# The state update of a linear-attention chunk moved ahead of the chunk's output product

## The chip, the cores and the metric

The kernel runs on one NeuronCore of one Trainium2 chip. The metric is the device time of one execution in microseconds (us), the median over the runs shown. The engines are named as in the profile: PE (TensorE matmul), PEld (its weight loads), DVE (VectorE), ACT (ScalarE), POOL (GpSimd), SP (SyncE, which issues most DMAs). A queue name such as SPq means the engine's instruction queue.

## The reference

One decoder layer on 2048 tokens of width 1024, with 16 learned meta tokens ahead of them. After an RMSNorm, one combined input projection feeds two branches, a state-space branch (SSD, 16 heads in 4 groups, chunks of 128) and a gated linear attention (GLA, 4 heads, key width 128, value width 256); both are projected, gated, added and projected once more. The two recurrences that matter here:

```python
# GLA, one chunk (per head): S has 128 x 256
o_inter = (q * exp(g)) @ S                  # uses the state before this chunk
o_intra = att @ v
S_new   = exp(g_last)[:, None] * S + k_dec.T @ v
o       = o_inter + o_intra
# SSD: the 16 meta tokens run first, as a chunk of their own; their final
# state is the initial state of the first real chunk
y_m, s_m = ssd_chunked(meta part, chunk=16, state0=0)
y_r, _   = ssd_chunked(real part, chunk=128, state0=s_m)
```

The gate of the GLA branch is `log_sigmoid(a_lr @ gla_gate_w2 + b) / 16`, with `gla_gate_w2` of 16 x 512. The reference uses chunks of 64 for GLA; the kernel uses 128, which gives the same sums.

## The kernel before

**First phase** (until about 1558 us): the 2048 tokens are taken in 4 blocks of 512, each as 4 chunks of 128; block 0 carries the meta tokens too. A block has eight units: four SSD groups, then four GLA heads. A unit is a projection (`ssd_proj`, `gla_proj`), long runs of 128x256 and 128x512 matmuls, which `yield`s after each piece; at its end it begins a scan (`ssd_scan`, `gla_scan`), a second generator. After each piece of projection, `step()` advances every running scan by one piece. So the PE's queue holds a piece of projection, one piece of each running scan, the next piece of projection, and so on. Weights are split in two parts (`accum` makes three matmuls of each product: high by high, high by low, low by high; lines 183 to 185). In block 0 each weight tile is loaded raw by SP, its high part is made by ACT (L163) and its low part by POOL (L164), and the result is saved to DRAM for later blocks (L179).

**Second phase**: gates, branch projections and the output projection, with seven products in place of eight.

**What sets the order.** PE's and SP's instructions stand in the order in which the code is written. The order on DVE, ACT and POOL is chosen at build time by a scheduler that works on its own estimates. All queues run in order: an instruction that waits holds back everything behind it on its engine. Waits are put in when the program is built, from the accesses to each tile. Each PSUM tile is one bank (128 x 512 f32); the pool `pc` has two, `pj` and `pt` three each.

**The GLA chunk** (`gla_scan`, L778 to 793). A chunk has one bank `po`: its right half gets the key product `kdt.T @ v` (three matmuls, L782 by way of 183 to 185), its left half the attention product `atp @ v` (three matmuls) and `qg @ s_gla` (L786). Then DVE reads the right half and updates `s_gla` in place (L787), and ACT reads the left half twice (L789, L791). A piece has two chunks, so a scan runs its four chunks in two pieces.

**Meta state** (`ssd_scan`, L512 to 517 and L580 to 588). In block 0 the piece that computes the meta state (L515, copied to SBUF by DVE L517) goes on, without a `yield`, into `before(1)` (transposes, L538) and `after(0)`, whose matmul L563 reads that state.

**Late constants** (L330 to 338). The GLA gate's weights `w2` and the masks `msk` are loaded by `late_constants()`: three DMAs of 16x512 (L333) into a tile of the tag `acc`, which has two buffers and which the convolution uses (L477 writes it, L481 reads it last), one DMA of the masks (L337), a copy on ACT (L334) and two instructions on DVE (L335, L338). It is called between the first and the second unit of block 0.

Of the kernel before, what the change touches and what calls it, by code (L numbers as in the profile page):

```python
# [7 lines left out]
F32 = mybir.dt.float32  # L8
# [4 lines left out]
ALU = mybir.AluOpType  # L13

P = 128
D = 1024
KT = 8
META = 16
BLK = 512
NCH = BLK // P  # L20
SG = 4
# [6 lines left out]
NACT = 8  # L28
# [12 lines left out]
def trunk_kernel(ctx: ExitStack, tc: tile.TileContext, xm, xmt, w_feat, w_tok, w_zm, w_br, w_o,  # L41
                 cf32, cmsk, pvec, fnw, hvec, gw2, out):
    nc = tc.nc
# [5 lines left out]
    def mk(pool, shape, dt, tag, **kw):  # L49
        cnt[0] += 1  # L50
        return pool.tile(shape, dt, tag=tag, name=f"{tag}_{cnt[0]}", **kw)
# [124 lines left out]
    def save(n):  # L176

        while len(unsaved) > n:
            nc.sync.dma_start(*unsaved.pop(0))  # L179

    def accum(ps, stat, mov, first, last, **kw):
        (sh, sl), (mh, ml) = stat, mov
        nc.tensor.matmul(ps, sh, mh, start=first, stop=False, **kw)  # L183
        nc.tensor.matmul(ps, sh, ml, start=False, stop=False, **kw)  # L184
        nc.tensor.matmul(ps, sl, mh, start=False, stop=last, **kw)  # L185
# [142 lines left out]
    msk = const.tile([P, NMSK, P], U8, name="msk")  # L328

    def late_constants():  # L330
        w2r = mk(wk, [P, META + BLK], F32, "acc")[:48, :512]
        for i in range(3):
            nc.sync.dma_start(w2r[16 * i:16 * i + 16, :], gw2)  # L333
        nc.scalar.activation(w2, w2r, AF.Copy)  # L334
        nc.vector.tensor_tensor(w2[32:48], w2r[32:48], w2[32:48].bitcast(F32), op=ALU.subtract)  # L335
        mstg = mk(wk, [P, D], F32, "tok4", bufs=NT4)[:, :NMSK * P]
        nc.sync.dma_start(mstg, cmsk)  # L337
        nc.vector.tensor_copy(msk.rearrange("p l t -> p (l t)"), mstg)  # L338
# [109 lines left out]
    def ssd_proj(o, g):  # L448
        m0, tt = o.m0, o.tt
        feats = []  # L450
        zs = mk(wk, [P, NCH, 256], F32, "tok4", bufs=NT4)
        if g == 0:
            pss = [bank(*pl) for pl in [(pj, "pj")] * 3 + [(pt, "pt")] + ([(pc, "pc")] if m0 else [])]
            yield from proj_tok("zm", w_zm, o.u, o.starts + [0] * o.ci0, list(enumerate(pss)), 288, 1, 256)
            begin(dt_chain(o, pss[NCH:] + pss[:NCH]))
            done = [(ps[:, :256], zs[:, c]) for c, ps in enumerate(pss[:NCH])]
        else:
            pss, places = halves_of(pj, "pj")
            yield from proj_tok(f"z{g}", w_tok[g], o.u, o.starts, places)
            done = [(ps, zs[:, 2 * r:2 * r + 2].rearrange("p c f -> p (c f)")) for r, ps in enumerate(pss)]  # L460
        for ps, dst in done:
            nc.scalar.activation(dst, ps, AF.Tanh, scale=0.5)
            nc.vector.scalar_tensor_tensor(dst, dst, 1.0, ps, op0=ALU.add, op1=ALU.mult)
        yield
        for j in range(4):
            ti = g * 4 + j
            pss = proj_feat(f"s{ti}", w_feat[T_SSD + ti], o.segs_all, o.mov)
            cin = mk(wk, [P, 3 + META + BLK], F32, "cin")
            acc = mk(wk, [P, META + BLK], F32, "acc")[:, :tt]
            nc.scalar.activation(cin[:, 0:3], tails[:, ti, :], AF.Copy)  # L470
            for ps, (a, n) in zip(pss, o.segs_all):
                nc.scalar.activation(cin[:, 3 + a:3 + a + n], ps[:, :n], AF.Copy)
                nc.scalar.activation(acc[:, a:a + n], ps[:, :n], AF.Identity, scale=hcw[:, ti, 3:4],  # L473
                                     bias=hcb[:, ti:ti + 1])
            nc.gpsimd.tensor_copy(tails[:, ti, :], cin[:, tt:tt + 3])
            for k in range(3):
                nc.vector.scalar_tensor_tensor(acc, cin[:, k:k + tt], hcw[:, ti, k:k + 1], acc,  # L477
                                               op0=ALU.mult, op1=ALU.add)
            f = mk(wk, [P, META + BLK], F32, "act", bufs=NACT)
            nc.scalar.activation(f[:, :tt], acc, AF.Tanh)  # L480
            nc.vector.scalar_tensor_tensor(f[:, :tt], f[:, :tt], 1.0, acc, op0=ALU.add, op1=ALU.mult)  # L481
            feats.append(f)
            yield
        begin(ssd_scan(o, g, feats, zs))

    cbs = {}
# [5 lines left out]
    def ssd_scan(o, g, feats, zs):  # L492
# [20 lines left out]
        def meta_state():  # L513
            ps = bank(pc, "pc")
            nc.tensor.matmul(ps[:, :256], btm[:META], xw[:META].rearrange("p a c -> p (a c)"),  # L515
                             start=True, stop=True)
            nc.vector.tensor_copy(s_ssd[:, g], ps[:, :256])  # L517
# [62 lines left out]
        yield  # L580
        if m0:
            meta_state()
        for c in range(1, NCH):
            before(c)
            after(c - 1)
            yield
# [15 lines left out]
    def gla_proj(o, h):  # L602
        m0 = o.m0
        t0 = T_GLA + 4 * h
        qs = mk(wk, [P, META + BLK], F32, "act", bufs=NACT)
        ps, = proj_feat(f"g{t0}", w_feat[t0], o.segs_real, o.mov)
        nc.scalar.activation(qs[:, :BLK], ps, AF.Copy, scale=QSCALE)
        yield
        kf = mk(wk, [P, META + BLK], F32, "act", bufs=NACT)
        for ps, (a, n) in zip(proj_feat(f"g{t0 + 1}", w_feat[t0 + 1], o.segs_all, o.mov), o.segs_all):  # L610
            nc.scalar.activation(kf[:, a:a + n], ps[:, :n], AF.Copy)
        yield
        vh = mk(wk, [P, NCH, 256], F32R, "tok4", bufs=NT4)
        vl = mk(wk, [P, NCH, 256], F32R, "tok4", bufs=NT4)
        vm = None
        pss, places = halves_of(pj, "pj")
        if m0:
            vm = mk(wk, [P, 256], F32, "c1", bufs=NC1)[:META]
            pv5 = bank(pt, "pt")
            places.append((2, pv5[:, :256]))  # L620
        yield from proj_tok(f"v{h}", w_tok[SG + h], o.u, o.starts + [0] * o.ci0, places)
        if m0:
            nc.scalar.activation(vm, pv5[:META, :256], AF.Copy)
        for r, ps in enumerate(pss):
            split(*[t[:, 2 * r:2 * r + 2].rearrange("p c f -> p (c f)") for t in (vh, vl)], ps)
        yield
        gs = []
        for j in range(2):
            ps, = proj_feat(f"g{t0 + 2 + j}", w_feat[t0 + 2 + j], o.segs_real, o.mov)
            gg = mk(wk, [P, BLK], F32, "gg", bufs=4)  # L630
            nc.scalar.activation(gg, ps, AF.Tanh, scale=0.5)
            nc.vector.scalar_tensor_tensor(gg, gg, 1.0, ps, op0=ALU.add, op1=ALU.mult)
            gs.append(gg)
            yield
        begin(gla_scan(o, h, qs, kf, (vh, vl), vm, gs))

    def gla_scan(o, h, qs, kf, vt, vm, gs):
# [140 lines left out]

        ot = mk(wk, [P, NCH, 256], F32, "ot", bufs=1)
        ssq = mk(sm, [P, 4], F32, "ssq")  # L780
        for c in range(NCH):
            po = bank(pc, "pc")  # L782
            vc = [t[:, c] for t in vt]
            accum(po[:, 256:], [t[:, c] for t in kdt], vc, True, True)
            accum(po[:, :256], [t[:, c] for t in atp], vc, True, False)
            nc.tensor.matmul(po[:, :256], qg[:, c * P:(c + 1) * P], s_gla[:, h], start=False, stop=True)  # L786
            nc.vector.scalar_tensor_tensor(s_gla[:, h], s_gla[:, h], egl[:, c:c + 1], po[:, 256:],  # L787
                                           op0=ALU.mult, op1=ALU.add)
            nc.scalar.activation(ot[:, c], po[:, :256], AF.Copy)  # L789
            jk = mk(wk, [P, 256], BF16, "junk", bufs=1)  # L790
            nc.scalar.activation(jk, po[:, :256], AF.Square, accum_out=ssq[:, c:c + 1])  # L791
            if c % 2:
                yield
# [19 lines left out]
    def step():  # L813
        running.extend(begun)
        begun.clear()
        for gen in list(running):
            if next(gen, running) is running:
                running.remove(gen)
# [7 lines left out]
    with tc.manual_schedule(engines={mybir.EngineType.PE, mybir.EngineType.SP}):  # L826
        for b in range(nblk):
            o = new_block(b, next_u[b])
            for i in range(SG + GH):
                if (b, i) in beside:  # L830
                    begin(beside_unit(beside[b, i]))
                if (b, i) == (0, 1):
                    late_constants()
                if i == 1:
                    begin(gates(o))
                if i == SG and b + 1 < nblk:
                    begin(fetch_u(b + 1))
                for _ in ssd_proj(o, i) if i < SG else gla_proj(o, i - SG):
                    step()
            save(0)  # L840
        while running or begun:
            step()
# [329 lines left out]
```

## Time and profile before

| what | value |
|---|---|
| time, median of 3 runs | 2348.6 us (2342.61 to 2350.83) |
| the profiled execution's own time | 2353.29 us |
| its span, first to last instruction | 2351.5 us |
| PE busy | 2251.0 us, 96% |
| DVE, ACT, POOL busy | 1547.5 (66%), 1181.6 (50%), 672.9 us (29%) |
| granted TensorE clock, mean | 0.982 |

The page of the profile gives busy time by engine and the costliest groups. A row of the waits reads: engine, line and tile of the instruction that waited, an arrow, what released it, then the total in us, how many times, and the longest. A row of the timeline reads: start, length, engine, line, operation, tile written, arrow, tiles read, shape, count, and in brackets the idle time of the engine just before it with its releaser. A row of the windows gives, for one stretch, its length, then busy time and number of instructions by engine, the granted TensorE clock (1.00 is full speed), the DMA share and GB/s. Matmul lengths overlap: in a run of 128x256 products one starts every 0.12 us and lasts 0.28 us.

### The profile page before, as it was taken

How to read it: one execution, taken by the hardware profiler on the slowest of the kernel's cores; microseconds unless marked ns; L12 is line 12 of the kernel's file. 1: busy time of each engine (PE TensorE's matmuls, PEld its weight loads, DVE VectorE, ACT ScalarE, POOL GpSimd, SP SyncE). 2: the span in 40 equal slices, each digit the busy share in tenths (PEclk: the TensorE clock that was granted, in tenths of full speed). 3: DMA queues.
4: the chain of work that ended last, by engine and by line, in shares of the span. 5: the costliest groups of instructions: out<-in, count | busy, mean ns of one | idle time of the engine just before them, and what ended most of it. 6: DMA issues, size and time to landing. Idle time of an engine off the chain costs nothing.

```text
span 2351.5 us, 36473 instructions
## 1 busy us (share of the span) xinstructions
PE 2251.0 (96%) x12641; PEld 1962.2 (83%) x12641; DVE 1547.5 (66%) x2895; ACT 1181.6 (50%) x2758; POOL 672.9 (29%) x681
## 2 busy tenths in 40 slices
PE   7799999999999999999999999879999999999998
PEld 7689889889888988888988898768878788888786
DVE  5576665676675567566568655674578854778866
ACT  5565655465534455543456443464455454554543
POOL 4343433122321212221122200207423354423331
PEclk9899999999999999999999999989999999999999
DMA  7665875666786676777677654447577876777753
GB/s 270 225 206 184 299 252 193 204 218 223 240 274 191 205 223 219 238 258 224 194 225 221 205 174 157 154 135 254 194 242 261 297 236 203 251 272 252 254 165 122
DMA packets 301545, 518.05 MB, mean 220 GB/s; under 512 B 27696, under 2 KB 143664, under 8 KB 301360
## 3 DMA queue, kind: packets, MB, share of 16 engines
q1 hardware_dynamic: 200400, 402.84, 52.9%
q10 hardware_dynamic: 100960, 112.88, 13.8%
q8 instruction: 99, 1.62, 0.3%
q14 instruction: 86, 0.70, 0.1%
HBM read 368.42 MB, written 147.19 MB: 219 GB/s over the span
## 4 chain that ended last, share of the span: by engine, by line
PE 48%; DMA 6%; DVE 6%; ACT 3%; issue 2%; SPq 1%; POOL 1%; ACTq 0%; DVEq 0%; POOLq 0%
PE pj L183 6%; PE pj L185 6%; PE pj L184 6%; PE psa L183 4%; PE psa L185 4%; PE psa L184 4%; PE psb L184 2%; PE psb L185 2%; PE psb L183 2%; DVE b L893 1%; DMA br<-br_t 1%; PE psc L183 1%; PE psc L185 1%; PE psc L184 1%; PE pc L562 1%
## 5 line engine op out<-in xcount | busy, mean ns | idle before, releaser
L183 PE MATMUL pj<-u,whl 128*128 128x512 f32 (+1 forms) x1184 | 447.9, 378 | 10.5 <-ACT whl L163 3.5
L185 PE MATMUL pj<-u,whl 128*128 128x512 f32 (+1 forms) x1184 | 431.8, 365 | 0.8 <-POOL whl L164 0.8
L184 PE MATMUL pj<-u,whl 128*128 128x512 f32 (+1 forms) x1184 | 430.8, 364 | 0.0
L183 PE MATMUL pj<-whl,u 128*128 128x256 f32 (+1 forms) x992 | 290.3, 293 | 8.2 <-ACT whl L163 6.7
L185 PE MATMUL pj<-whl,u 128*128 128x256 f32 (+1 forms) x992 | 283.4, 286 | 1.5 <-DVE u L298 1.4
L184 PE MATMUL pj<-whl,u 128*128 128x256 f32 (+1 forms) x992 | 283.4, 286 | 1.0 <-POOL whl L164 1.0
L183 PEld LDWEIGHTS pj<-u,whl 128*128 128x128 f32 x1184 | 225.9, 191 | 48.8 <-ACT whl L163 3.9
L183 PE MATMUL psa<-b,a 128*128 128x512 f32 x640 | 249.8, 394 | 11.1 <-ACT sn L930 8.2
L185 PEld LDWEIGHTS pj<-u,whl 128*128 128x128 f32 x1184 | 224.9, 190 | 36.9 <-POOL whl L164 1.1
L184 PEld LDWEIGHTS pj<-u,whl 128*128 128x128 f32 x1184 | 225.5, 190 | 33.6
L185 PE MATMUL psa<-b,a 128*128 128x512 f32 x640 | 251.3, 393 | 1.2 <-DVE a L914 1.2
L184 PE MATMUL psa<-b,a 128*128 128x512 f32 x640 | 251.0, 392 | 0.0
L183 PEld LDWEIGHTS pj<-whl,u 128*128 128x128 f32 x992 | 191.2, 193 | 9.4 <-ACT whl L163 6.9
L184 PEld LDWEIGHTS pj<-whl,u 128*128 128x128 f32 x992 | 191.0, 193 | 2.1 <-POOL whl L164 1.6
L185 PEld LDWEIGHTS pj<-whl,u 128*128 128x128 f32 x992 | 190.8, 192 | 2.2 <-DVE u L298 2.2
L893 DVE TENSOR_TENSOR b<-br,b 128x512 fp32r<-128x512 f32 x196 | 153.1, 804 | 56.2 <-ACT b L892 55.7
L80 POOL TENSOR_TENSOR wr<-wr 128x256 f32<-128x256 f32 x80 | 65.1, 814 | 425.5 <-DMA wr<-y 169.7
L904 POOL TENSOR_TENSOR as<-ar,ar 128x512 f32<-128x512 f32 x40 | 57.8, 1446 | 447.5 <-DMA ar<-in_w_br 191.2
L164 POOL TENSOR_TENSOR whl<-wr,whl 128x512 fp32r<-128x512 f32 (+1 forms) x100 | 132.9, 1335 | 182.5 <-ACT whl L163 155.2
L892 ACT ACTIVATE b<-br 128x512 fp32r<-128x512 f32 x196 | 119.2, 626 | 112.3 <-DMA br<-br_t 41.5
L914 DVE TENSOR_TENSOR a<-ar,a 128x512 fp32r<-128x512 f32 x160 | 131.8, 839 | 64.4 <-ACT a L913 64.1
L477 DVE SCALAR_TENSOR_TENSOR acc<-cin,hcw,acc 128x512 f32<-128x512 f32 (+1 forms) x192 | 154.6, 805 | 27.0 <-ACT acc L473 26.3
(271 smaller groups left out, 5062.7 us busy)
## 6 DMA issues: line engine op xcount, KB each, us to landing
whl<-k_s SPq DMA_DIRECT2D x96, 512.0 KB, 4.5
whl<-k_g SPq DMA_DIRECT2D x96, 512.0 KB, 4.2
whl<-k_v SPq DMA_DIRECT2D x48, 512.0 KB, 3.7
whl<-k_z SPq DMA_DIRECT2D x36, 512.0 KB, 3.8
wr<-in_w_feat SPq DMA_DIRECT2D x64, 256.0 KB, 4.2
k_s<-whl SPq DMA_DIRECT2D x32, 512.0 KB, 3.7
cb<-cumd ACTq DMA_DIRECT2D x64, 256.0 KB, 5.4
y<-gg ACTq DMA_DIRECT2D x64, 256.0 KB, 4.5
```

The source lines that it names most:

```text
L80: nc.gpsimd.tensor_tensor(o, x, y, op=ALU.subtract)
L164: nc.gpsimd.tensor_tensor(hl[:, 1], raw, hl[:, 0].bitcast(F32), op=ALU.subtract)
L183: nc.tensor.matmul(ps, sh, mh, start=first, stop=False, **kw)
L184: nc.tensor.matmul(ps, sh, ml, start=False, stop=False, **kw)
L185: nc.tensor.matmul(ps, sl, mh, start=False, stop=last, **kw)
L477: nc.vector.scalar_tensor_tensor(acc, cin[:, k:k + tt], hcw[:, ti, k:k + 1], acc, op0=ALU.mult, op1=ALU.add)
L562: nc.tensor.matmul(py[:, h * 64:(h + 1) * 64], dm[:, h], xdt[:, h], start=True, stop=True)
L892: nc.scalar.activation(t[:, 0], raw, AF.Copy)
L893: nc.vector.tensor_tensor(t[:, 1], raw, t[:, 0].bitcast(F32), op=ALU.subtract)
L904: nc.gpsimd.tensor_tensor(s1, a21, a22, op=ALU.add)
L914: nc.vector.tensor_tensor(t[:, 1], src, t[:, 0].bitcast(F32), op=ALU.subtract)
```

## The change

Three edits. In the GLA chunk, the DVE update is issued right after the key product, and it writes a second buffer `st`; the two buffers change roles with each chunk, and the chunk's `qg` product reads the old one. In block 0's SSD scans, the meta state is a piece of its own (a `yield` more). `late_constants()` is called within the first unit of block 0, after that unit's second piece, and its staging tile takes a buffer of the tag `act` (eight buffers).

```diff
     def late_constants():
-        w2r = mk(wk, [P, META + BLK], F32, "acc")[:48, :512]
+        w2r = mk(wk, [P, META + BLK], F32, "act", bufs=NACT)[:48, :512]
...
         if m0:
             meta_state()
+            yield
         for c in range(1, NCH):
             before(c)
             after(c - 1)
...
         ot = mk(wk, [P, NCH, 256], F32, "ot", bufs=1)
         ssq = mk(sm, [P, 4], F32, "ssq")
+        states = [s_gla[:, h], mk(wk, [P, 256], F32, "st", bufs=1)]
         for c in range(NCH):
             po = bank(pc, "pc")
             vc = [t[:, c] for t in vt]
+            old, new = states[c % 2], states[1 - c % 2]
             accum(po[:, 256:], [t[:, c] for t in kdt], vc, True, True)
+            nc.vector.scalar_tensor_tensor(new, old, egl[:, c:c + 1], po[:, 256:], op0=ALU.mult, op1=ALU.add)
             accum(po[:, :256], [t[:, c] for t in atp], vc, True, False)
-            nc.tensor.matmul(po[:, :256], qg[:, c * P:(c + 1) * P], s_gla[:, h], start=False, stop=True)
-            nc.vector.scalar_tensor_tensor(s_gla[:, h], s_gla[:, h], egl[:, c:c + 1], po[:, 256:],
-                                           op0=ALU.mult, op1=ALU.add)
+            nc.tensor.matmul(po[:, :256], qg[:, c * P:(c + 1) * P], old, start=False, stop=True)
             nc.scalar.activation(ot[:, c], po[:, :256], AF.Copy)
...
-                if (b, i) == (0, 1):
-                    late_constants()
...
-                for _ in ssd_proj(o, i) if i < SG else gla_proj(o, i - SG):
+                for n, _ in enumerate(ssd_proj(o, i) if i < SG else gla_proj(o, i - SG)):
                     step()
+                    if (b, i, n) == (0, 0, 1):
+                        late_constants()
```

In the changed kernel lines move by one or two: L787 is L788 there, L786 is L790, L654 is L655, L659 is L660, L681 is L682, L789 and L791 are L791 and L793.

**PE at the second chunk of the first GLA scan.** Each row is an instruction with its output and inputs; in brackets stands the engine on whose counter it waits (`DVE_49` counts DVE's instructions, `PE_49` PE's own, `Activation_49` ACT's). Before:

```order
L183 MATMUL pc_4101<-tok_455_3080,kdt_3665 128x256 [waits PE_49]
L184 MATMUL pc_4101<-tok_456_3081,kdt_3665 128x256
L185 MATMUL pc_4101<-tok_455_3080,kdt_3666 128x256
L183 MATMUL pc_4101<-tok_455_3080,atp_3983 128x256 [waits Activation_49]
L184 MATMUL pc_4101<-tok_456_3081,atp_3983 128x256
L185 MATMUL pc_4101<-tok_455_3080,atp_3984 128x256 [waits DVE_49]
L786 MATMUL pc_4101<-s_gla,act_3555 128x256 [waits DVE_49]
```

And of the change:

```order
L183 MATMUL pc_4102<-tok_451_3064,kdt_3649 128x256 [waits PE_49]
L184 MATMUL pc_4102<-tok_452_3065,kdt_3649 128x256
L185 MATMUL pc_4102<-tok_451_3064,kdt_3650 128x256
L183 MATMUL pc_4102<-tok_451_3064,atp_3983 128x256 [waits DVE_49,Activation_49]
L184 MATMUL pc_4102<-tok_452_3065,atp_3983 128x256
L185 MATMUL pc_4102<-tok_451_3064,atp_3984 128x256
L790 MATMUL pc_4102<-st_4089,act_3548 128x256
```

The matmuls are the same. L786's wait for the previous chunk's update is gone; the first attention product (the second L183) now waits for DVE. The count for which it waits is reached by L788, the update of the same chunk; it is so in all 64 chunks.

**DVE around the same scan's updates.** Before:

```order
L681 TENSOR_TENSOR sq_4367<-g_all_384 128x512 [waits DVE_49]
L787 SCALAR_TENSOR_TENSOR s_gla<-s_gla,egl_3553,pc_4089 128x256 [waits PE_49]
L654 TENSOR_TENSOR act_4113<-act_4113,act_3567 128x528 [waits Activation_49]
L787 SCALAR_TENSOR_TENSOR s_gla<-s_gla,egl_3553,pc_4101 128x256 [waits PE_49]
L659 TENSOR_TENSOR act_4125<-act_4125,act_3489 128x512 [waits Activation_49]
L787 SCALAR_TENSOR_TENSOR s_gla<-s_gla,egl_3553,pc_4204 128x256 [waits PE_49]
```

And of the change:

```order
L682 TENSOR_TENSOR sq_4368<-g_all_384 128x512 [waits DVE_49]
L788 SCALAR_TENSOR_TENSOR st_4089<-s_gla,egl_3546,pc_4090 128x256 [waits PE_49]
L655 TENSOR_TENSOR act_4114<-act_4114,act_3560 128x528 [waits Activation_49]
L788 SCALAR_TENSOR_TENSOR s_gla<-st_4089,egl_3546,pc_4102 128x256 [waits DVE_49,PE_49]
L660 TENSOR_TENSOR act_4126<-act_4126,act_3472 128x512 [waits Activation_49]
L788 SCALAR_TENSOR_TENSOR st_4089<-s_gla,egl_3546,pc_4205 128x256 [waits DVE_49,PE_49]
```

The updates stand at the same places of DVE's queue: behind the next head's decay work (L682), and with an instruction between them that waits for ACT (L655).

**ACT in the first unit of block 0**, where the first projection's outputs (`pj`, `pt`, `pc`) are read and the next weights (`whl`) are split. Before:

```order
L163 ACTIVATE whl_522<-wr_524 128x288 [waits DMAHW0_49,DMAHW5_49,PE_49,Pool_49]
L163 ACTIVATE whl_591<-wr_593 128x512 [waits DMAHW4_49,DMAHW7_49,PE_49,Pool_49]
L462 ACTIVATE tok_39_386<-pj_387 128x256 [waits PE_49]
L462 ACTIVATE tok_39_386<-pj_388 128x256 [waits PE_49]
L373 ACTIVATE alr_385<-pj_387 128x48 [waits DVE_49]
```

And of the change:

```order
L334 ACTIVATE w_374<-act_589 48x512 [waits DMAHW7_49,DMAHW6_49,DMAHW0_49]
L462 ACTIVATE tok_39_386<-pj_387 128x256 [waits PE_49]
L462 ACTIVATE tok_39_386<-pj_388 128x256 [waits PE_49]
L373 ACTIVATE alr_385<-pj_387 128x48 [waits DVE_49]
L462 ACTIVATE tok_39_386<-pj_389 128x256 [waits PE_49]
L373 ACTIVATE alr_385<-pj_388 128x48 [waits DVE_49]
L462 ACTIVATE tok_39_386<-pt_390 128x256 [waits PE_49]
L373 ACTIVATE alr_385<-pj_389 128x48 [waits DVE_49]
L373 ACTIVATE alr_385<-pt_390 128x48 [waits DVE_49]
L373 ACTIVATE alr_385<-pc_391 128x48 [waits DVE_49]
L377 ACTIVATE de_578<-dx_567 128x80
L163 ACTIVATE whl_600<-wr_602 128x512 [waits DMAHW4_49,DMAHW3_49,Pool_49]
```

The copy of `w2` (L334) stands where the split of the next weight tile (`whl_591` before, `whl_600` now) stood; that split is now behind all reads of the first projection. On SP the four DMAs of `late_constants` now stand ahead of the first of these weight tiles' loads.

## The prediction

> **What bounds the kernel now.** First the page: the span and the busy time by engine.
>
> ```profile
> span 2351.5 us, 36473 instructions
> PE 2251.0 (96%) x12641; PEld 1962.2 (83%) x12641; DVE 1547.5 (66%) x2895; ACT 1181.6 (50%) x2758; POOL 672.9 (29%) x681
> ```
>
> PE is busy for 2251.0 of 2351.5 us, so only 100.5 us of idle time can be won, and whatever makes PE wait anew is paid almost in full. Next the waits of PE, of which three rows belong to the three edits: weights that came late (10.1), the GLA product that waited for the state (5.6) and the SSD product that waited for the meta state (5.3).
>
> ```profile
> PE pj L183 <- ACT whl L163: 10.1, 2, 6.7
> PE pc L786 <- DVE s_gla L787: 5.6, 4, 3.0
> PE pc L563 <- DVE s_ssd L517: 5.3, 1, 5.3
> ```
>
> The wait that the first edit attacks is small: 5.6 us in 4 of 64 chunks. Why it is so small shows in an undisturbed chunk of the timeline:
>
> ```profile
> 434.63 0.28 PE L185 MATMUL pc<-tok,kdt 128*128 128x256 f32 x1
> 434.75 0.28 PE L183 MATMUL pc<-tok,atp 128*128 128x256 f32 x1
> 435.10 0.60 PE L786 MATMUL pc<-s_gla,act 128*128 128x256 f32 x2
> 435.35 0.47 PE L183 MATMUL pc<-tok,kdt 128*128 128x256 f32 x1
> 435.74 0.48 DVE L787 SCALAR_TENSOR_TENSOR s_gla<-s_gla,egl,pc 128x256 f32<-128x256 f32 x1 [3.04 <-PE pc L786]
> 436.27 0.70 PE L786 MATMUL pc<-s_gla,act 128*128 128x256 f32 x2
> ```
>
> DVE updates the state (435.74 to 436.22) while PE runs the next chunk's six products, and L786 needs the state only at 436.27. The update lies beside PE's work. The next view is that of line 787 itself:
>
> ```profile
> L787 DVE SCALAR_TENSOR_TENSOR s_gla<-s_gla,egl,pc x64: 462/480/482, 339.1 to 1551.6; 128x256 f32<-128x256 f32 x64
>   PE pc L786: 73.5, 38
>   ACT ot L789: 21.6, 25
> ```
>
> The second row: in 38 of 64 chunks DVE had been idle before the update; in the other 26 it came to it late. The third: ACT's copy of `po` waited 25 times for this update, though it reads the left half of the bank and the update the right half and `s_gla`. So accesses to one bank are kept in the order of the program, also when they touch different halves.
>
> **Edit 1, the state update.** In the new order DVE reads the right half of `po` before the attention product writes the left half. By the rule that the third row shows, that product must then wait for DVE; and PE's new order shows it, a wait on DVE at the first attention product, in all 64 chunks. What was beside PE's work is put between two of its products. Behind the waiting matmul stand the rest of the chunk, the next chunk of the piece and the next projection.
>
> The price where DVE is free: the key product ends at 434.63 + 0.28 = 434.91; DVE answers 0.04 us after PE's end (L786 ends at 435.70, L787 starts at 435.74); the update takes 0.48; and PE resumes 0.06 us after DVE's end, as at the first scan, where DVE ends at 339.58:
>
> ```profile
> 336.24 0.28 PE L185 MATMUL pc<-tok,kdt 128*128 128x256 f32 x1
> 338.50 0.69 DVE L681 TENSOR_TENSOR sq<-g_all 128x512 f32<-128x512 f32 x1
> 339.11 0.47 DVE L787 SCALAR_TENSOR_TENSOR s_gla<-s_gla,egl,pc 128x256 f32<-128x256 f32 x1
> 339.64 0.70 PE L786 MATMUL pc<-s_gla,act 128*128 128x256 f32 x2 [1.63 <-DVE s_gla L787]
> 339.99 0.47 PE L183 MATMUL pj<-u,whl 128*128 128x264 f32 x1
> ```
>
> So the attention product starts at 434.91 + 0.04 + 0.48 + 0.06 = 435.49 in place of 434.75: 0.74 us. After a wait PE starts again slower: L786 takes 339.99 - 339.64 = 0.35 us to the next matmul's start, and 435.35 - 435.10 = 0.25 in flow, 0.10 more. I take 0.84, and 0.74 as the lower end: 64 x 0.84 = **+54** (47 at least).
>
> The price where DVE is late is more. DVE's queue is in order, and the updates stand in it behind the next head's decay work, with L655 between the first two, which waits for ACT. The second scan shows both:
>
> ```profile
> 385.55 0.28 PE L185 MATMUL pc<-tok,kdt 128*128 128x256 f32 x1
> 385.71 1.66 DVE L681 TENSOR_TENSOR sq<-g_all 128x512 f32<-128x512 f32 x1
> 387.29 0.47 DVE L787 SCALAR_TENSOR_TENSOR s_gla<-s_gla,egl,pc 128x256 f32<-128x256 f32 x1
> 390.06 0.71 DVE L654 TENSOR_TENSOR act<-act,act 128x528 f32<-128x528 f32 x1 [2.31 <-ACT act L653]
> 390.69 0.47 DVE L787 SCALAR_TENSOR_TENSOR s_gla<-s_gla,egl,pc 128x256 f32<-128x256 f32 x1
> ```
>
> The first key product ends at 385.83, but DVE comes at 387.29, 1.4 us later than a free DVE would; the second update sits behind L654 until 390.69. At the first scan DVE came at 339.11, when the key product had ended at 336.52, 2.6 us late. Before, PE saw such lateness 4 times; now it sees all of it. For the 26 late chunks I take 1.0 us each, between half of a decay instruction (0.69/2 = 0.35) and 2.6: **+26** (9 to 68). Nearer the lower end, because after a first wait DVE has caught up.
>
> The clock. The windows show what PE's idle time does to the granted clock (the clock is the third number from the end, 1.00 is full speed; the first pair after the length is PE's busy time and matmuls):
>
> ```profile
> 634.90:638.30 3.40, 1.51 (x11) 1.46 (x12) 2.69 (x6) 2.34 (x6) 2.26 (x3) 0.99 0.70 213
> 638.30:641.70 3.40, 3.40 (x16) 3.22 (x15) 2.77 (x8) 2.14 (x8) 1.47 (x2) 0.51 0.97 370
> 296.90:300.30 3.40, 1.56 (x14) 1.56 (x15) 2.02 (x2) 3.02 (x8) 3.40 (x3) 1.00 0.48 155
> 300.30:303.70 3.40, 3.40 (x31) 3.40 (x30) 3.07 (x6) 1.64 (x4) 0.58 (x1) 1.00 1.00 354
> ```
>
> After 3.4 us with 1.51 us of PE work the next 3.4 us ran at 0.51; after 1.56 us of work they ran at full clock. So a piece that idles for some 1.85 of 3.4 us also pays half of 3.4, 1.7 us. A piece's two waits where DVE is free leave about 2 x 0.6 = 1.2 us of idle, not enough; a late DVE adds the rest. I take 8 of the 32 pieces: **+14** (none, to all 32 with 54).
>
> Removed: L786's waits, **-5.6**. The writes to a second buffer and ACT's earlier start cost and win nothing: ACT is busy for 50%, and the bank that it frees is used two chunks later.
>
> [...]
>
> **Edit 2, the meta state.** The gap before L563, and what followed:
>
> ```profile
> 102.01 0.39 DVE L517 COPY s_ssd<-pc 128x256 f32<-128x256 f32 x1
> 102.46 0.80 PE L563 MATMUL pc<-s_ssd,act 128*128 128x256 f32 x1 [5.33 <-DVE s_ssd L517]
> 102.50:105.70 3.20, 3.20 (x11) 2.84 (x12) 2.96 (x8) 1.59 (x4) 0.78 (x1) 0.50 0.31 108
> ```
>
> The copy was late behind DVE's scans. With the `yield`, a piece of projection, 47 matmuls of 0.12 us by PE's new order, is put between: 5.6 us, which covers 5.33. I take all of it and the half clock behind it (3.2/2 = 1.6): **-7** (0 to -7; what is late next is the same scan's later pieces). The three other groups had no such wait, and get nothing.
>
> **Edit 3, the late constants.** SP waited for a buffer of `acc`, and the weights behind it came late:
>
> ```profile
> SPq L333 <- DVE act L481: 15.6, 1, 15.6
> 66.42 0.58 PE L183 MATMUL pj<-whl,u 128*128 128x256 f32 x1 [6.66 <-ACT whl L163]
> 67.82 0.58 PE L184 MATMUL pj<-whl,u 128*128 128x256 f32 x1 [0.82 <-POOL whl L164]
> 69.70 0.58 PE L184 MATMUL pj<-whl,u 128*128 128x256 f32 x1 [0.23 <-POOL whl L164]
> 66.40:71.60 5.20, 4.13 (x16) 3.55 (x17) 0.00 (x0) 1.26 (x2) 3.49 (x3) 0.50 0.99 366
> ```
>
> 6.66 + 0.82 + 0.23 = 7.7 us of gaps, and 5.2 us at half clock, 2.6 more: **-10.3** (at least -5, if something else in that queue is late). But the call's new place has a price. On ACT the split of the first weight tile of the next projection now stands behind all reads of the first one:
>
> ```profile
> 30.92 0.63 ACT L163 ACTIVATE whl<-wr 128x512 fp32r<-128x512 f32 x1 [2.28 <-PE pj L184]
> 31.63 1.29 POOL L164 TENSOR_TENSOR whl<-wr,whl 128x512 fp32r<-128x512 f32 x1 [2.10 <-ACT whl L163]
> 35.30 0.28 ACT L377 ACTIVATE de<-dx 128x80 f32<-128x80 f32 x1
> 33.74 0.37 PE L183 MATMUL pj<-u,whl 128*128 128x264 f32 x1
> ```
>
> PE used that tile at 33.74. L377 came at 35.30, with two splits ahead of it that now stand behind it. If it ends and the split starts at about 35.0, its low part is there at 35.0 + 0.63 + 1.29 = 36.9: a new gap of 3, and 1.7 of clock: **+4.7** (0 if ACT gets through earlier, 6 if the masks' DMA on SP delays the tile too).
>
> **Sum.** 54 + 26 + 14 - 5.6 - 7 - 10.3 + 4.7 = +75.8 on a profiled execution of 2353.29 us. That execution lies 4.7 above the median of the runs; set on the median of 2348.6 the sum gives **2424 us**, 3.2% slower.
>
> **Rivals.** (a) *The update really leaves the path.* If the attention product did not in fact wait for DVE, only the gains were left: -5.6 - 7 - 10.3 + 4.7 = -18, **2330 us**, faster. It decides if the wait for L788 costs less than 18/64 = 0.28 us a chunk. Against it: the update alone takes 0.48, and the order names the wait. For it: only that DVE is idle before 38 updates, which shortens nothing below 0.74. [...] Chance 4%. That the edits cancel to no change: 2%.
>
> (b) *Only the floor is paid.* DVE's lateness shrinks since PE's waits let it catch up, and the clock holds: 54 + 9 - 5.6 - 7 - 10.3 + 4.7 = +45, **2394 us**. For it: the 38 of 64. Against: L654's wait for ACT, which PE's waiting does not shorten. 22%.
>
> (c) *The clock falls at every piece.* Two waits close together in 3.4 us with 256-column products may count as idle enough: 32 x 1.7 = 54 in place of 14, **2464 us**. For it: in the 1.56 us window full clock was held only just. Against: a pair's 1.2 us is well short of 1.85. 16%.
>
> My forecast, 2405 to 2445, has 56%.
>
> **How the numbers follow.** Faster by over 0.3% (7 us, about what a measurement of this kernel tells from no change): 4%; within it 2%; slower 94%. The range takes in most of (b) and of (c): from 2380 (the lower ends, 47 + 9 - 5.6 - 7 - 10.3 = +33) to 2470 ((c), with 6 us more for lateness).
>
> **What would show it.** A row of PE's waits for L788 at L183 (64 waits or nearly, some 60 to 90 us with the gaps of 0.6 us each and a few of 2 to 4); L790 without a wait; the gaps at 66 and 102 us gone, one of about 3 us near 34; more slices with a lower PEclk in the first phase; the second phase (from about 1560 us before) unchanged in length. The forecast is wrong if these waits are short or few, or if the second phase moves too.

## The result, and the profile after

The changed kernel takes **2418.3 us** (median, 2411.1 to 2422.1) against 2345.6 us (2342.6 to 2350.8) of the kernel before on the same chip: a ratio of **1.0305, 95% interval 1.0281 to 1.033**. It is slower, as forecast (2424 us, 2405 to 2445 for the likeliest case). The profiled execution took 2417.06 us.

The head of the page of the changed kernel, with the span and the busy times:

```profile
span 2415.3 us, 36595 instructions
PE 2275.5 (94%) x12641; PEld 1975.7 (82%) x12641; DVE 1564.0 (65%) x2895; ACT 1185.4 (49%) x2758; POOL 677.8 (28%) x681
```

The matmuls are as many as before (12641), yet PE is busy for 24.5 us longer. The span grew by 63.8, so the other 39.3 us are idle time. Next the waits of PE after the change:

```profile
PE pc L183 <- DVE st L788: 43.5, 32, 8.4
PE pc L183 <- DVE s_gla L788: 18.0, 28, 1.3
...
PE pc L183 <- ACT junk L793: 5.0, 4, 1.8
```

The attention product's first matmul waits for the state update L788 in 60 of 64 chunks, 61.5 us in all. The other four waits at that place are put on ACT's L793, 5.0 us; two of them are 0.67 us long, as long as many waits for the update. The three rows that the edits went after (L786 for L787, L563 for L517, and `whl`) are gone from the top.

Where in the program the time went shows when the span is cut at the first GLA key product and at the first product of the second phase. The first block is the kernel before, the second the changed one; busy times and counts stand in the order PE, PEld, DVE, ACT, POOL.

```profile
0.00:336.00 336.00, 295.47 (x2082) 276.08 (x2083) 216.87 (x417) 192.89 (x480) 132.74 (x130) 0.96 0.71 241
336.00:1558.80 1222.80, 1184.81 (x7200) 1052.88 (x7198) 774.99 (x1698) 601.96 (x1563) 248.47 (x320) 0.98 0.65 207
1558.80:2351.50 792.70, 770.76 (x3360) 633.25 (x3360) 555.59 (x781) 386.78 (x716) 291.65 (x232) 0.99 0.69 232
```
```profile
0.00:319.05 319.05, 291.61 (x2082) 274.16 (x2083) 218.77 (x417) 193.13 (x480) 136.03 (x130) 0.98 0.74 253
319.05:1618.40 1299.35, 1212.01 (x7200) 1069.12 (x7198) 782.36 (x1699) 605.90 (x1563) 250.97 (x320) 0.96 0.60 195
1618.40:2415.30 796.90, 771.85 (x3360) 632.38 (x3360) 562.87 (x781) 386.38 (x716) 290.75 (x232) 0.99 0.68 230
```

The part up to the first key product, where edits 2 and 3 lie, is 17.0 us shorter. The part with the GLA chunks is **76.6 us longer** with the same 7200 matmuls: 27.2 us more busy time, at a lower mean clock (0.96 against 0.98), and 49.4 us more idle time. The second phase is 4.2 us longer.

An undisturbed piece of two chunks on PE, before the change, from its first key product to the next matmul that is not of the scan:

```profile
345.98 0.28 PE L183 MATMUL pc<-tok,kdt 128*128 128x256 f32 x1
346.33 0.28 PE L183 MATMUL pc<-tok,atp 128*128 128x256 f32 x1
...
347.47 0.28 PE L183 MATMUL pc<-tok,atp 128*128 128x256 f32 x1
...
348.39 0.27 PE L709 MATMUL pt<-cst,act 128*16 128x128 f32 x1
```

and the same piece after it:

```profile
334.91 0.28 PE L183 MATMUL pc<-tok,kdt 128*128 128x256 f32 x1
...
335.14 0.28 PE L185 MATMUL pc<-tok,kdt 128*128 128x256 f32 x1
335.99 0.39 PE L183 MATMUL pc<-tok,atp 128*128 128x256 f32 x1 [0.57 <-DVE st L788]
...
337.97 0.39 PE L183 MATMUL pc<-tok,atp 128*128 128x256 f32 x1 [0.57 <-DVE s_gla L788]
...
338.86 0.27 PE L710 MATMUL pt<-cst,act 128*16 128x128 f32 x1
```

The piece took 348.39 - 345.98 = 2.41 us and takes 338.86 - 334.91 = 3.95. That is 1.54 for two chunks, 0.77 each; from one attention product to the next it is 337.97 - 335.99 = 1.98 against 347.47 - 346.33 = 1.14 before, 0.84 more. Of the 28 two-chunk pieces ahead of the last two scans, nineteen look like this one. In the other nine DVE comes late, as in the second scan, shown here on DVE and PE of the changed kernel:

```profile
376.16 1.64 DVE L682 TENSOR_TENSOR sq<-g_all 128x512 f32<-128x512 f32 x1
377.72 0.47 DVE L788 SCALAR_TENSOR_TENSOR st<-s_gla,egl,pc 128x256 f32<-128x256 f32 x1
380.49 0.71 DVE L655 TENSOR_TENSOR act<-act,act 128x528 f32<-128x528 f32 x1 [2.30 <-ACT act L654]
381.12 0.47 DVE L788 SCALAR_TENSOR_TENSOR s_gla<-st,egl,pc 128x256 f32<-128x256 f32 x1
```
```profile
376.01 0.28 PE L185 MATMUL pc<-tok,kdt 128*128 128x256 f32 x1
378.33 0.35 PE L183 MATMUL pc<-tok,atp 128*128 128x256 f32 x1 [2.05 <-DVE st L788]
...
381.74 0.55 PE L183 MATMUL pc<-tok,atp 128*128 128x256 f32 x1 [1.32 <-DVE s_gla L788]
```

The key product was done at 376.29, but DVE stood in the next head's decay work (L682) until about 377.8. The second update stood behind L655, which itself waited 2.30 us for ACT. PE now sees both delays, and at 381.74 its matmuls already run slower (0.55 in place of 0.39).

### The profile page after: what moved, and what is told of

It reads as the page before. It is cut to its first block, busy times and chain, and to the rows that moved or that the text cites. A ratio compares the mean times of both kernels' runs of the same rounds, so it can differ in the third digit from the quotient of the medians.

```text
span 2415.3 us, 36595 instructions
## 1 busy us (share of the span) xinstructions
PE 2275.5 (94%) x12641; PEld 1975.7 (82%) x12641; DVE 1564.0 (65%) x2895; ACT 1185.4 (49%) x2758; POOL 677.8 (28%) x681
## 5 line engine op out<-in xcount | busy, mean ns | idle before, releaser
L183 PE MATMUL pj<-u,whl 128*128 128x512 f32 (+1 forms) x1184 | 451.1, 381 | 15.5 <-ACT acc L473 6.4
L183 PE MATMUL pj<-whl,u 128*128 128x256 f32 (+1 forms) x992 | 290.8, 293 | 1.5 <-ACT u L296 1.5
L183 PEld LDWEIGHTS pj<-u,whl 128*128 128x128 f32 x1184 | 228.1, 193 | 54.8 <-ACT acc L473 7.5
L183 PE MATMUL psa<-b,a 128*128 128x512 f32 x640 | 250.3, 395 | 13.7 <-ACT sn L932 10.7
L185 PEld LDWEIGHTS pj<-u,whl 128*128 128x128 f32 x1184 | 227.2, 192 | 37.3 <-POOL whl L164 1.4
L184 PEld LDWEIGHTS pj<-u,whl 128*128 128x128 f32 x1184 | 228.1, 193 | 33.6
L183 PEld LDWEIGHTS pj<-whl,u 128*128 128x128 f32 x992 | 191.4, 193 | 3.2 <-ACT u L296 2.0
```

## The experiments

Four kernels ran beside one set of runs of the kernel before (2351.3 us), four others beside another (2350.3); ratios are to those. The intervals are 95%.

**1. Edit 1 undone, edits 2 and 3 kept.** Is the whole loss edit 1's?

```diff
...
+            nc.tensor.matmul(po[:, :256], qg[:, c * P:(c + 1) * P], s_gla[:, h], start=False, stop=True)
+            nc.vector.scalar_tensor_tensor(s_gla[:, h], s_gla[:, h], egl[:, c:c + 1], po[:, 256:],
+                                           op0=ALU.mult, op1=ALU.add)
```

> Edits 2 and 3 kept, edit 1 undone. Theory (edit 1 costs, by the order of accesses to one PSUM bank; edits 2 and 3 gain what the first 336 us showed, 17 us): 2345.6 - 17 = 2329 us, between 2322 and 2335. Rival (the gain at the start is given back later, PE only comes earlier to the next late transfer): 2340 to 2347.

Measured: 2333.7 us, **0.9922 [0.9899, 0.9945]**. The whole loss and more is edit 1's: without it the other two edits make the kernel about 18 us faster. This is about what rival (a) would have given. The part with the chunks, in the windows:

```profile
324.90:1540.90 1216.00, 1181.23 (x7200) 1048.74 (x7198) 778.58 (x1699) 601.41 (x1563) 249.94 (x320) 0.99 0.65 208
```

1216.0 us, 83 less than in the changed kernel.

**2. Edit 1 alone.**

```diff
+        states = [s_gla[:, h], mk(wk, [P, 256], F32, "st", bufs=1)]
...
+            nc.vector.scalar_tensor_tensor(new, old, egl[:, c:c + 1], po[:, 256:], op0=ALU.mult, op1=ALU.add)
             accum(po[:, :256], [t[:, c] for t in atp], vc, True, False)
...
```

> Edit 1 alone, edits 2 and 3 undone. Theory (the edits add up): 2345.6 + 90 = 2435 us, or 2345.6 + 77 = 2423 if only the stage of the chunks counts; 2420 to 2438. Rival (a part of the loss comes from edits 2 and 3, whose scans now run into the chunks later): below 2410.

Measured: 2437.1 us, **1.0356 [1.0322, 1.0391]**, +84 us by the ratio. The waits for the update at L183 are 57.0 us in all, against 61.5 in the changed kernel:

```profile
PE pc L183 <- DVE st L787: 38.3, 31, 7.4
PE pc L183 <- DVE s_gla L787: 18.7, 28, 2.0
```

So edit 1 costs about as much without the other two edits as with them; the intervals show no difference.

**3. The changed kernel, with the key product in a bank of its own.** Order, second buffer and update stay where the change put them. If the wait comes from the shared bank, it must go; if the early place of the update in DVE's queue is what hurts, it must stay.

```diff
             po = bank(pc, "pc")
+            pk = bank(pt, "pt")[:, :256]
...
-            accum(po[:, 256:], [t[:, c] for t in kdt], vc, True, True)
-            nc.vector.scalar_tensor_tensor(new, old, egl[:, c:c + 1], po[:, 256:], op0=ALU.mult, op1=ALU.add)
+            accum(pk, [t[:, c] for t in kdt], vc, True, True)
+            nc.vector.scalar_tensor_tensor(new, old, egl[:, c:c + 1], pk, op0=ALU.mult, op1=ALU.add)
```

> The changed kernel, but the key product of each chunk goes to a bank of its own (pool pt), so that no two engines meet in one bank at the update. Theory (the wait is one of bank order): all 64 waits of the attention product for the update go, with lateness and clock, and the 5.6 us of the old waits stay away: 2345.6 - 17 - 6 = 2323, up to 2335 if the pt banks come late. Rival (the loss comes from the new order of DVE's and ACT's queues, or from the second buffer): it stays above 2400.

Measured: 2329.4 us, **0.9908 [0.9886, 0.9931]**, faster than both kernels. PE's waits for the update are now at L791, the `qg` product, which needs the state, and no longer at the attention product:

```profile
PE pc L791 <- DVE st L789: 8.0, 6, 2.8
```

The part with the chunks, cut at the same two events:

```profile
319.20:1534.40 1215.20, 1177.74 (x7201) 1047.90 (x7199) 782.80 (x1698) 601.13 (x1563) 253.79 (x320) 0.99 0.65 209
```

1215.2 us in place of 1299.4: the 84 us are the shared bank. The same piece of two chunks, on PE and on DVE:

```profile
328.92 0.28 PE L183 MATMUL pt<-tok,kdt 128*128 128x256 f32 x1
329.27 0.28 PE L183 MATMUL pc<-tok,atp 128*128 128x256 f32 x1
...
331.19 0.27 PE L710 MATMUL pt<-cst,act 128*16 128x128 f32 x1
```
```profile
329.47 0.48 DVE L789 SCALAR_TENSOR_TENSOR st<-s_gla,egl,pt 128x256 f32<-128x256 f32 x1 [4.03 <-PE pt L185]
```

DVE updates from 329.47 to 329.95 while the attention product, started at 329.27, runs: the piece is back at 2.27 us. Against experiment 1 the intervals overlap, and both keep some 8 us of waits for a late update (here 6 times; there, in the old order, 5 times). So even in a bank of its own the early update gains nothing that these runs can tell: what it could have removed was DVE's lateness, and DVE's queue is as late as before.

**4. Six matmuls more in the wait.** If an undisturbed chunk waits for 0.77 to 0.84 us, PE can do six products of 0.12 us there for nothing. Six copies of the key product go into a spare bank, and nothing reads them.

```diff
+            pf = bank(pt, "pt")[:, :256]
+            for _ in range(2):
+                accum(pf, [t[:, c] for t in kdt], vc, True, True)
             accum(po[:, :256], [t[:, c] for t in atp], vc, True, False)
```

> The changed kernel with six more matmuls (the key product twice again, into a bank that nobody reads) between the key product and the attention product of each chunk: 6 x 0.12 = 0.72 us of PE work a chunk, 46 us in all, whose results are not used. Theory (PE idles there for 0.74 us or more): the added work costs nothing; and since PE no longer idles, the half clock goes, so 2404 to 2412 us, 14 below the change at most. If the clock has no share: 2418 to 2425. Rival (PE does not really wait there): 2418 + 46 = 2464.

Measured: 2405.3 us, **1.0232 [1.0206, 1.0259]**: with 384 matmuls more it is faster than the change (1.0281 to 1.033). The same piece:

```profile
335.81 0.28 PE L183 MATMUL pc<-tok,kdt 128*128 128x256 f32 x1
...
336.90 0.38 PE L183 MATMUL pc<-tok,atp 128*128 128x256 f32 x1
...
339.76 0.27 PE L710 MATMUL pt<-cst,act 128*16 128x128 f32 x1
```

339.76 - 335.81 = 3.95, to the hundredth the length with the empty wait. What is left of the waits are late updates, 10 in place of 60:

```profile
PE pc L183 <- DVE st L788: 23.3, 10, 6.4
```

The part with the chunks in the windows:

```profile
320.10:1608.90 1288.80, 1240.63 (x7585) 1106.48 (x7583) 785.74 (x1699) 604.39 (x1563) 251.36 (x320) 0.98 0.62 197
```

The part with the chunks is 10.6 us shorter than the changed kernel's, and its clock is 0.98 in place of 0.96. By the clock's records 92.7 us of this part of the changed kernel ran at half clock, and PE worked for 71.9 of them. Here a mean of 0.98 (0.975 to 0.985) over 1288.8 us leaves 39 to 64 us at half clock; with the same share of work in them, an estimate, that is 30 to 50 us of work. At half clock the changed kernel's 128x256 products start every 0.21 us in place of 0.12, so at most half of the difference, 11 to 21 us, is time won back; the part is 10.6 us shorter. The waits thus cost clock beside their own length, and filling them brings a part of it back.

**5. Both chunks' key products ahead of both attention products.** Two banks of `pc`, a third state buffer; the two updates have more of PE's work beside them. In this kernel three small tiles (`ss2`, `gl`, `egl`) also have two buffers in place of four; what that costs was not measured.

```diff
...
+            if c % 2 == 0:
+                for d in (c, c + 1):
+                    pos[d] = bank(pc, "pc")
+                    accum(pos[d][:, 256:], [t[:, d] for t in kdt], [t[:, d] for t in vt], True, True)
...
+                    nc.vector.scalar_tensor_tensor(new, old, egl[:, d:d + 1], pos[d][:, 256:],
+                                                   op0=ALU.mult, op1=ALU.add)
+            po = pos[c]
```

> The changed kernel with the key products and updates of both chunks of a piece ahead of both attention products (same banks, one state buffer more). Theory (what is paid is the time from a key product to the end of its update, less the PE work between): the first attention product has one key product, 0.36 us, as cover and still waits about 0.4 to 0.5 us; the second update is covered by the first chunk's products. 32 x 0.45 = 14 in place of 54, and a part of the lateness: 25 to 30 above the version with a bank of its own (2329), so 2345 to 2362, a ratio of 0.998 to 1.005 to the kernel before. Rival (the order of DVE's queue and the second buffer cost, not the bank): above 2400.

Measured: 2364.7 us, **1.0059 [1.0043, 1.0076]**, a little above what was expected. Where DVE is free, one wait of 0.22 to 0.32 us is left of a pair:

```profile
337.44 0.39 PE L183 MATMUL pc<-tok,atp 128*128 128x256 f32 x1 [0.22 <-DVE st L791]
```

but the late updates stay, and now hold up a pair at once:

```profile
PE pc L183 <- DVE st L791: 31.8, 29, 6.6
327.47 0.55 PE L183 MATMUL pc<-tok,atp 128*128 128x256 f32 x1 [3.50 <-DVE st L791]
```

The kernel is 35 us slower than with the own bank. Work in between takes most of the floor (the wait that is paid even where DVE is free) away; only a bank of its own keeps the late updates from holding up the attention product.

**6. Edit 2 alone.**

```diff
             meta_state()
+            yield
```

> Edit 2 alone. Prediction's term: 7 us faster, ratio 0.997. Rival: the gaps of 3.5 and 2.1 us at 238 and 299 us, which also went in the run with edits 2 and 3, belong to this edit: 12 to 15 us faster, ratio 0.994 to 0.995.

Measured: 2341.7 us, **0.9967 [0.9954, 0.9981]**, 7.7 us faster. The gap before L563 is gone, and so are two later ones that the kernel before had in the same block:

```profile
238.01 0.39 PE L183 MATMUL pj<-u,whl 128*128 128x264 f32 x1 [3.49 <-ACT whl L163]
298.74 0.33 PE L714 MATMUL pt<-cst,act 128*128 128x128 f32 x1 [2.10 <-ACT gg L598]
```

In return the weights' gap of edit 3 is longer in this run (6.66 before):

```profile
68.33 0.58 PE L183 MATMUL pj<-whl,u 128*128 128x256 f32 x1 [8.41 <-ACT whl L163]
```

**7. Edit 3 alone.**

```diff
-        w2r = mk(wk, [P, META + BLK], F32, "acc")[:48, :512]
+        w2r = mk(wk, [P, META + BLK], F32, "act", bufs=NACT)[:48, :512]
...
+                    if (b, i, n) == (0, 0, 1):
+                        late_constants()
```

> Edit 3 alone. Prediction's terms: -10.3 + 4.7 = 5.6 us faster, ratio 0.9976, with the gaps at 66 us gone and a new one of about 2.5 us near 35 us. Rival: the gaps at 238 and 299 us belong to this edit: 11 to 14 us faster, ratio 0.994 to 0.995.

Measured: 2348.3 us, **0.9988 [0.9973, 1.0003]**, 2.8 us faster, with an interval from 6.3 faster to 0.7 slower: not told apart from no change. The gaps at 66 us are gone, and the foreseen new one is there, in two pieces of 1.61 and 0.54 us, shorter than the 3 that were forecast:

```profile
36.82 0.58 PE L183 MATMUL pj<-u,whl 128*128 128x264 f32 x1 [1.61 <-ACT whl L163]
```

The gap before L563 stays (4.55 us), as edit 2 is missing here. Edits 2 and 3 alone give 7.7 and 2.8, together (experiment 1) 18 us. The intervals (3 to 5 us to each side) leave room for most of the 7.5 between; whether the two edits help each other is not settled.

**8. The own bank, and the constants one piece later.** Experiment 3 with `late_constants()` after the third piece of the first unit and its tile in a buffer of `sq`, to remove the new gap near 35 us.

```diff
-        w2r = mk(wk, [P, META + BLK], F32, "act", bufs=NACT)[:48, :512]
+        w2r = mk(wk, [P, BLK], F32, "sq", bufs=NSQ)[:48, :512]
...
-                    if (b, i, n) == (0, 0, 1):
+                    if (b, i, n) == (0, 0, 2):
```

> The version with a bank of its own, and the late constants called one piece later with their staging tile in the tag sq, which is free by then, so that the split of the next weights stands ahead of the first projection's reads on ACT again. Theory (the new gap of 2.4 us at 35 us and half a clock window behind it are the price of the new place): 4 us faster than the version with a bank of its own, 2325 us, ratio 0.989. Rival (the weights come late at another place): the same, 0.991.

Measured: 2331.6 us, **0.9916 [0.9898, 0.9934]**. The new gap, 1.60 and 0.83 us in experiment 3, shrinks to 0.53 us,

```profile
34.62 0.39 PE L183 MATMUL pj<-u,whl 128*128 128x264 f32 x1 [0.53 <-ACT alr L373]
```

but the time cannot be told from experiment 3's (0.9908). The profiled execution, 2320.5 us of span, was at the low end of its runs; no gain is claimed from it.

## Why the prediction was right, point by point

**The mechanism** was right, and experiment 3 shows it: the attention product waits for an update that reads the other half of its bank, in every chunk, and in a bank of its own the wait and the loss are gone. Rival (a), chance 4%, falls: the wait costs 0.77 us and more where it had to be under 0.28.

**The floor, 64 x 0.84 = 54.** An undisturbed piece is 1.54 to 1.68 us longer (2.41 to 3.95; others 2.22 to 3.90), so 0.77 to 0.84 a chunk, 49 to 54 for 64 chunks. The working, from three durations of the trace before, held. Experiment 4 measured it a second way: work of 6 x 0.12 us per chunk fits in without lengthening the piece.

**DVE late, 26 x 1.0 = 26.** Too high by some 5, and otherwise made up. 51 of the 64 gaps at the attention product are the floor's, 31.2 us in all, 0.61 each; 13 are longer, 35.2 us in all, so 27.3 above the floor's. They were half as many, each twice as long (2.1). The count of 26 came from the updates before which DVE had not been idle; a DVE that comes busy from one instruction to the next need not be late. And not all of the 27.3 is new: at the last scans of the kernel before, PE had waited for the attention operand itself, 6.8 us in three gaps, of which the first is

```profile
1518.89 0.58 PE L185 MATMUL pc<-tok,atp 128*128 128x256 f32 x1 [4.29 <-DVE atp L232]
```

In the changed kernel one wait for the update stands in their place:

```profile
1574.39 0.55 PE L183 MATMUL pc<-tok,atp 128*128 128x256 f32 x1 [8.36 <-DVE st L788]
```

New lateness is therefore 27.3 - 6.8 = 20.5.

**The clock, 8 x 1.7 = 14.** The size was about right, the picture not, so the size is in part luck. PE's busy time in this part grew by 27.2; the floor's share of that is 64 x (0.77 to 0.84 less the 0.61 of idle time), 10 to 15, and leaves 12 to 17 for the clock. By the clock's records PE worked for 71.9 us of this part at half clock, 33.5 before; half of the difference bounds the loss at 19. But of the nine falls beside projections six lasted 6.8 us, not the 3.4 that the term took, and about a third of the loss is in the last scans, with no projection left to fill PE. The windows over those, of the kernel before and of the changed one:

```profile
1514.00:1560.00 46.00, 27.31 (x118) 21.78 (x117) 34.00 (x69) 21.91 (x62) 9.32 (x7) 0.74 0.13 46
```
```profile
1570.00:1620.00 50.00, 32.31 (x115) 24.91 (x116) 30.25 (x66) 21.38 (x60) 4.93 (x5) 0.57 0.06 24
```

About as many matmuls take 5.0 us more of PE, at a mean clock of 0.57 against 0.74. Rival (c) came true in these last scans only. In the scans before them it falls: the nineteen undisturbed pieces, with two waits of 0.57 to 0.67 us each, ran at full clock (1.00). Rival (b) falls too, since lateness and clock were both paid.

**Removed, -5.6.** The waits of L786 are gone, and the part's other gaps are 4.7 us shorter in all. So the part has 49 to 54 for the floor, 20.5 for lateness, 12 to 17 for the clock, less 10.3: about the 76.6 between the two traces, where the forecast had 54 + 26 + 14 - 5.6 = 88. Other pairs of traces that differ by edit 1 alone lie on both sides: this part is 1216.0 us long in experiment 1, 83 less than in the changed kernel, and 1291.3 in experiment 2, 68.5 more than in the kernel before. The profiled execution of experiment 2 was the fastest of its four, and that of the kernel before (2353.3) lay above its five timed runs (2342.6 to 2350.8), so 68.5 and 76.6 are rather too small. The timed runs say 84 (76 to 92, experiment 2), which leaves room for 88.

**Edit 2, -7.** Experiment 6 gives -7.7 [-10.8, -4.5], so the size was right. The reason given, 5.33 of gap and 1.6 of clock, is not the whole of it: two later gaps of 5.6 us in all went as well, and another grew.

**Edit 3, -10.3 + 4.7 = -5.6.** Experiment 7 gives -2.8, and its interval takes in both -5.6 and nothing. In the changed kernel the new gap is 1.61 + 0.84 = 2.45 us of PE's time, where about 3 was forecast, since the split started at 34.60, not at 35.0. PE takes up its work when the high part is there and stops again for the low part, which POOL ended at 36.58 (the second row is the weight load for which the matmul waits):

```profile
35.28 0.39 PE L183 MATMUL pj<-u,whl 128*128 128x264 f32 x1 [1.61 <-ACT whl L163]
...
36.63 0.19 PEld L185 LDWEIGHTS pj<-u,whl 128*128 128x128 f32 x1 [1.05 <-POOL whl L164]
```

The clock fell behind it as forecast, for 3.4 us from 37.45 by its records. Together the two edits shorten the part before the first key product by 17.0 in the changed kernel's trace and by 11.1 in experiment 1's, whose profiled execution was the slowest of its six; -12.6 was forecast, and the timed runs say 18 (13 to 24, experiment 1). The gaps at 238 and 299 us, 5.6 in all, which the forecast had not counted, are about the difference between forecast and timed runs.

**The second phase** was to be unchanged in length and is 4.2 us longer (792.7 to 796.9). Over the kernels of the experiments, none of which touches it, it was 791.6 to 796.0; nothing points to a cause in the change, and it stays open whether any of it is the change's.

In the timed runs the change costs 2418.3 - 2345.6 = 72.7 us, forecast were 75.8. By the experiments edit 1 costs 84 alone, or 90 as the difference between the changed kernel and experiment 1 ((1.0305 - 0.9922) x 2348), where 88 was forecast; edits 2 and 3 win 18 in place of 12.6. The term that was off by the largest share of its size is the gain of these two. That the total came within 3 us is in part luck: the sum was built on the profiled execution of the kernel before, and from that one to the profiled execution of the changed kernel the time grows by only 2417.1 - 2353.3 = 63.8; the medians, which single executions miss by several us, lie 72.7 apart.

## What to carry to other kernels

Before an operand's reader is moved ahead of a product, look at which bank of PSUM the two share: accesses to one bank followed the order of the program here even in different halves, so an early read put 0.8 us between two matmuls and laid bare every delay of the reader's queue, and a bank of its own turned +3.1% into -0.9%. A wait of 5.6 us in 4 of 64 places did not say that the update stood at a bad place; it said that DVE's queue was late there, and after the move it was as late as before. The price of such a wait is its floor times its count, plus the lateness of the queue that answers, plus the clock that the idle time costs; here the clock weighed most, for each wait, in the last scans, where no other work was left to fill PE.

## What the runs showed of the hardware

More work made the kernel faster: 384 matmuls that nothing reads took 0.7% off the time, since PE did them in time that it had spent waiting, and the part with the chunks ran at a mean clock of 0.98 in place of 0.96. Two stretches of the changed kernel, each with the one that followed it, show how little it takes; the second is the piece with two waits shown above:

```profile
375.38:378.78 3.40, 1.35 (x10) 1.09 (x9) 2.77 (x5) 1.31 (x4) 1.38 (x1) 1.00 0.44 139
378.78:382.18 3.40, 2.08 (x9) 1.62 (x8) 1.69 (x3) 3.35 (x11) 0.60 (x1) 0.50 0.50 147
334.90:338.30 3.40, 2.25 (x15) 1.79 (x14) 0.96 (x2) 1.87 (x6) 1.28 (x1) 1.00 0.70 243
338.30:341.70 3.40, 3.40 (x30) 3.25 (x29) 1.81 (x6) 1.95 (x7) 1.26 (x1) 1.00 0.68 222
```

After 1.35 us of work in 3.4 the next 3.4 ran at half clock, after 2.25 at full clock. No gap in the first stretch was longer than 2.05 us. In the traces of the kernel before and of the changed one the clock's records, apart from the last one of each, last whole multiples of 3.41 us. Cut into such stretches, from 31 us on, all 29 stretches at full clock with less than 1.52 us of PE work were followed by half clock, and none with more than 1.70 us was; between these, 3 of 6 were, and what decides there stays open. Gaps of PE shorter than one stretch were enough here, and what the rows follow is the share of work in a stretch.
